# MoE input rows stored with the columns 8 apart side by side; pair 0 alone gathered on TensorE, pair 1 fetched by DMA

## The chip, the cores and the metric

One core of a Trainium2 chip runs the whole program. The metric is device microseconds of one execution; smaller is better.

## What is computed

The reference is a trunk of two decoder layers over 512 tokens of 1024 features in float32. Each layer has a token mixer and then a mixture of experts (MoE). The change lies in the MoE, cut here to what matters:

```
h  = rmsnorm(x) * (1 + scale) + shift            # (512, 1024), scale and shift from the conditioning
group  = argmax of 4 group logits                # top-1 group
expert = top-2 of the 8 experts in that group, weights by softmax
for each chosen expert e:                        # 32 experts, hidden width 256
    y += weight * (silu(h @ w_gate[e]) * (h @ w_up[e])) @ w_down[e]
x = x + gate * y
```

Every token goes to two of 32 experts, so an expert sees some 32 of the 512 tokens.

## The kernel before

**Tiling.** The tokens are four tiles of 128 (NT = 4). The feature axis is 8 chunks of 128 (NK = 8): feature d = 8q + k belongs to chunk k on partition q, which is the order in which the expert weights lie in memory. Every expert has 64 slots for its rows, two experts make a pair, and a pair's 128 slots fill the partitions. There are 16 pairs a layer, counted from 0.

**Routing.** `mix_out` runs the last stage of the mixer tile by tile and, woven into it, the router: `route_turn` and `route_mm` (logits), `route_sum` (L1478 and L1480, the logits turned), `route_pick` (L1499 to L1517, the chosen experts, `sel`), `route_rank` (L1524 and L1525, each row's place within its expert), `route_place` (L1530 and L1569, a 0/1 matrix `P` of token against slot), `route_send` (L1538 to L1547, the token number is written to a list in memory), `route_scale` (POOL, L1446: `h` = x times a row of factors), `route_halves` (L1607 and L1608: norm and shift). For the last of the four tiles these steps stand in an order written out by hand (L1389 to L1414).

**Two ways to the input of a pair.** Pairs 0 and 1 get their input `X` from TensorE: `gather_tile` multiplies `h` of each token tile, 8 column-strided chunks as the stationary operand, with `P` of four experts (256 columns moving), adding up over the tiles in four PSUM banks (L1588); ACT copies these to `X` (L1663). The other pairs are fetched: `fetch` clears a tile `raw` on POOL (L1629) and issues an indirect DMA that collects the pair's rows (L1630); `turn` transposes them on TensorE, eight 128x128 blocks read with a stride of 8 columns (L1712), and ACT copies them to `X` (L1713). One `fetch(h)` brings two pairs, 2h and 2h+1, and is called when `turn` has used up the earlier two. Before the first fetch the lists of token numbers are read back (`idx`, L1558).

**The pairs.** `gate_up(n)` (L1728) is 32 matmuls in two halves of the feature axis, followed by the activation (DVE L1737 to L1743, ACT L766 to L770). `down(n)` (L1763) is 16 matmuls, the scaling on DVE (L1766) and a scatter by POOL (L1776), or for the last pairs an addition on the chip (L1769 to L1804). The loop does `gate_up(n)`, `down(n-1)`, `turn(n+1)`. Behind `gate_up(0)` stands `overflow`, a conditional branch for experts with over 64 rows: every engine takes part in it, and none of its body is executed here. Instructions of SP that stand behind it are issued once SP has passed it.

**Loads.** Weights come through SP in the order of `plan_loads`: for pair 0 `gu`, pair 1 `gu`, pair 0 `dn`, pair 2 `gu`, pair 1 `dn` and so on (`gu` = the gate and up weights in four 1 MB tiles, `dn` = the down weights in two). All large tiles, weights, `X` and `raw`, share one pool of 19 buffers of 1 MB that is used in rotation, so each load waits for the release of the tile 19 allocations earlier. Up to the branch 16 weight tiles are loaded: pairs 0, 1 and 2 `gu`, pairs 0 and 1 `dn`. The loads behind it take, in this order, three buffers of pair 0's `gu`, then those of pair 1's `gu` and of the first `X`, then pair 0's `dn`. Near the end of a layer the rows that were scattered are loaded back (`yt`) between pair 14's and pair 15's weights.

## Time and profile before

| | |
|---|---|
| median of 3 runs | 1343.57 us (1343.27 to 1343.91) |
| the profiled execution | 1342.48 us, of which the span of the trace is 1340.7 us |
| mean granted TensorE clock | 0.941 of full speed |
| busy share of the span | PE 87%, PE weight loads 54%, DVE 54%, ACT 30%, POOL 27% |
| bytes moved | 350.95 MB, mean 262 GB/s |
| gate and up matmuls, L1728 | 260.0 us in 1024 instructions |
| gather matmuls, L1588 | 35.1 us in 128 instructions |
| transposes of fetched rows, L1712 | 33.8 us in 224 instructions (groups of four) |

The first layer's MoE runs from about 405 to 681 us of the span, the second's from about 1052 to 1326 us. A share of the span says little here, because the mixer and the MoE have different limits; the readings that matter are taken inside the two MoE stages, at their start and their end.

### The profile page before, as it was taken

How to read it: one execution, taken by the hardware profiler on the slowest of the kernel's cores; microseconds unless marked ns; L12 is line 12 of the kernel's file. 1: busy time of each engine (PE TensorE's matmuls, PEld its weight loads, DVE VectorE, ACT ScalarE, POOL GpSimd, SP SyncE). 2: the span in 40 equal slices, each digit the busy share in tenths (PEclk: the TensorE clock that was granted, in tenths of full speed). 3: DMA queues.
4: the chain of work that ended last, by engine and by line, in shares of the span. 5: the costliest groups of instructions: out<-in, count | busy, mean ns of one | idle time of the engine just before them, and what ended most of it. 6: DMA issues, size and time to landing. Idle time of an engine off the chain costs nothing. (4 is left out here: it accounts for less than half of the span.)

```text
span 1340.7 us, 16646 instructions
## 1 busy us (share of the span) xinstructions
PE 1164.4 (87%) x5900; PEld 728.2 (54%) x5902; DVE 719.9 (54%) x1573; ACT 401.6 (30%) x1029; POOL 358.0 (27%) x302
## 2 busy tenths in 40 slices
PE   4888899999988997788859998999998999888795
PEld 2766566666764553344337765767576644334342
DVE  3786877776662121124676576887777321112276
ACT  3442422545322111111134333345352121111113
POOL 0251322461232121111052313346132321111100
PEclk9898989989989999999979997989999999888898
DMA  9973256462877999999962220463385899999982
GB/s 379 400 276 116 75 189 225 145 228 56 312 237 267 411 413 410 405 398 411 393 225 95 75 95 30 176 219 111 107 273 209 247 412 413 412 411 404 398 336 79
DMA packets 104860, 350.95 MB, mean 262 GB/s; under 512 B 16874, under 2 KB 27882, under 8 KB 90434
## 3 DMA queue, kind: packets, MB, share of 16 engines
q1 hardware_dynamic: 85936, 313.31, 61.5%
q10 hardware_dynamic: 10738, 22.24, 4.8%
q0 software_dynamic: 8096, 14.24, 2.9%
q8 instruction: 51, 0.84, 0.3%
q14 instruction: 39, 0.32, 0.1%
HBM read 333.35 MB, written 29.48 MB: 271 GB/s over the span
## 5 line engine op out<-in xcount | busy, mean ns | idle before, releaser
L1728 PE MATMUL pa<-w,X 128*64 128x512 f32 x1024 | 260.0, 610 | 43.3 <-DMA w<-w_up 35.2
L1728 PEld LDWEIGHTS pa<-w,X 128*64 128x64 f32 x1024 | 102.2, 139 | 163.9 <-issue 119.5
L1763 PE MATMUL pb<-w,hT 128*64 128x512 f32 x512 | 142.7, 658 | 11.1 <-ACT hT L1752 10.7
L736 PE MATMUL pa<-wp,hhi 128*128 128x512 f32 x320 | 136.3, 429 | 3.5 <-ACT hhi L638 3.4
L737 PE MATMUL pa<-wp,hhi 128*128 128x512 f32 x320 | 131.7, 412 | 0.9 <-DVE wp L241 0.9
L738 PE MATMUL pa<-wp,hlo 128*128 128x512 f32 x320 | 130.1, 408 | 0.8 <-DVE hlo L639 0.8
L1737 DVE TENSOR_SCALAR sg<-pa 128x256 f32<-128x256 f32 x32 | 13.6, 424 | 201.9 <-PE pa L1728 201.9
L241 DVE TENSOR_TENSOR wp<-w,wp 128x1024 fp32r<-128x1024 f32 (+1 forms) x68 | 90.1, 1333 | 36.5 <-ACT wp L240 36.1
L1776 POOL DMA_INDIRECT yd<-y,idx x24 | 24.0, 1000 | 308.9 <-DVE y L1766 246.6
L240 ACT ACTIVATE wp<-w 128x1024 fp32r<-128x1024 f32 (+1 forms) x72 | 72.2, 1014 | 97.7 <-PE pa L738 44.7
L1763 PEld LDWEIGHTS pb<-w,hT 128*64 128x64 f32 x512 | 49.4, 149 | 80.3 <-issue 52.7
L1713 ACT ACTIVATE X<-pa 128x512 f32<-128x512 f32 x56 | 31.9, 598 | 171.8 <-PE pa L1712 157.8
L736 PEld LDWEIGHTS pa<-wp,hhi 128*128 128x128 f32 x320 | 63.0, 198 | 28.3 <-issue 6.5
L766 ACT ACTIVATE sge<-sg 128x256 f32<-128x256 f32 x32 | 13.2, 413 | 204.2 <-DVE sg L1737 204.2
L1766 DVE TENSOR_TENSOR y<-pb,gbc 128x512 f32<-128x512 f32 x48 | 33.2, 692 | 76.3 <-PE pb L1763 58.1
L738 PEld LDWEIGHTS pa<-wp,hlo 128*128 128x128 f32 x320 | 63.1, 197 | 17.0 <-issue 1.7
L737 PEld LDWEIGHTS pa<-wp,hhi 128*128 128x128 f32 x320 | 63.2, 198 | 15.2 <-DVE wp L241 1.9
L915 POOL TENSOR_TENSOR QX<-E,qk 128x1024 f32<-128x1024 f32 x16 | 40.9, 2559 | 98.4 <-ACT E L913 59.0
L1335 PE MATMUL pa<-wp,mlo 128*128 128x512 f32 x128 | 51.9, 406 | 1.0 <-DVE mlo L1307 1.0
L1333 PE MATMUL pa<-wp,mhi 128*128 128x512 f32 x128 | 52.6, 411 | 0.2
L931 PE MATMUL pb<-QX,E 64*128 64x128 f32 x448 | 43.5, 295 | 9.6 <-DVE hkg L1008 5.3
L1334 PE MATMUL pa<-wp,mhi 128*128 128x512 f32 x128 | 51.1, 399 | 0.0
(350 smaller groups left out, 2185.6 us busy)
## 6 DMA issues: line engine op xcount, KB each, us to landing
w<-w_gate SPq DMA_DIRECT2D x128, 512.0 KB, 13.8
w<-w_up SPq DMA_DIRECT2D x128, 512.0 KB, 7.6
w<-w_down SPq DMA_DIRECT2D x64, 1024.0 KB, 11.3
w<-w_ada SPq DMA_DIRECT2D x48, 1024.0 KB, 10.2
w<-w_in SPq DMA_DIRECT2D x16, 1024.0 KB, 6.8
w<-w_in SPq DMA_DIRECT2D x16, 512.0 KB, 7.0
yd<-Sblk SPq DMA_DIRECT2D x8, 1024.0 KB, 17.9
w<-w_out SPq DMA_DIRECT2D x8, 1024.0 KB, 6.3
```

The lines of the kernel that those rows point to most:

```text
L240: keep(self.S.activation(hi, w[:, sl, :], AF.Copy))
L241: keep(self.lo_engine.tensor_tensor(lo, w[:, sl, :], hi.bitcast(F32), op=OP.subtract))
L736: T.matmul(acc[i], hh[:, s], wh, start=k == 0, stop=False)
L737: T.matmul(acc[i], hh[:, s], wl, start=False, stop=False)
L738: T.matmul(acc[i], hl[:, s], wh, start=False, stop=k == NK - 1)
L915: G.tensor_tensor(qx, e, qk[i][:, pr, None, :].to_broadcast([P, 8, P]), op=OP.mult)
L931: T.matmul(o, e[r, lv, :], qx[r, lv, :], start=True, stop=True)
L1333: T.matmul(acc, mh[kh][:, kk, s], hi[:, kk % 2, :], start=first, stop=False)
L1334: T.matmul(acc, mh[kh][:, kk, s], lo[:, kk % 2, :], start=False, stop=False)
L1335: T.matmul(acc, ml[kh][:, kk, s], hi[:, kk % 2, :], start=False, stop=last)
L1728: mm = T.matmul(p[j * 64:j * 64 + 64, :], X[h][:, kh * 4 + kk, ep * P + j * 64:ep * P + j * 64 + 64], w[j][:, :, kk], start=kh == 0 and kk ...
L1763: T.matmul(p[j * 64:j * 64 + 64, :], hT[:, f, j * 64:j * 64 + 64], w[j][:, f, cs], start=f == 0, stop=f == 1)
```

## The change

Row storage: `h` is written in the order "k q" instead of "q k", so that the 128 columns of a chunk lie side by side. `route_scale` does the turning on POOL: it reads x and the factors with a stride of 8 columns, in runs of 64, and writes side by side. The shift row is turned once a layer by a new ACT copy of 128x1024 (`shift`), which takes a fifth buffer of the tag that holds the four `h`. The gather's stationary operand and the transposes of fetched rows then read 128 neighbouring columns.

Pairs: only pair 0 goes through the gather. `P` has 128 columns, there are two PSUM banks and two copies to `X`, and two opening matmuls instead of four. Pair 1 is fetched: `fetch(r)` brings pairs 2r+1 and 2r+2, clears both halves first and issues both DMAs behind that; the last fetch brings pair 15 alone. There are 15 gathers of rows a layer instead of 14. `down(0)` stands right behind the branch, before `turn(1)`, instead of behind `gate_up(1)`. In the written order of the last tile, `route_sum` stands before `gather_tile(0)`, and `gather_tile(2)` behind `route_send` of the last tile. The loads of pair 0's `dn` move ahead of pair 1's `gu`.

```diff
-                if e0 > 0:
-                    for e in (e0 - 2, e0 - 1):
-                        self.plan(("dn", l, e))
+                for e in (0, 1) if e0 == 0 else (e0 - 2, e0 - 1) if e0 > 2 else ():
+                    self.plan(("dn", l, e))
...
         self.route_rank(last - 1)
+        self.route_sum(last)
         self.gather_tile(0)
-        self.route_sum(last)
         self.route_pick(last)
...
         self.route_rank(last)
-        self.gather_tile(2)
         self.route_place(last)
         self.route_group(last)
         self.route_send(l, last)
+        self.gather_tile(2)
         self.gather_tile(last)
...
+        self.shift = self.t4([P, D], F32, "shift")
+        self.S.activation(self.shift.rearrange("p (k q) -> p k q", k=NK), self.rows[:, 0].rearrange("p (q k) -> p k q", k=NK), AF.Copy)
...
-        self.G.tensor_tensor(self.h[i][:, cs], self.xt[i][:, cs], self.rows[:, 1, cs], op=OP.mult)
+        h, x, s = self.h[i][:, cs], self.xt[i][:, cs], self.rows[:, 1, cs]
+        if self.turned:
+            h = self.h[i].rearrange("p (k q) -> p k q", k=NK)[:, :, half * 64:half * 64 + 64]
+            x, s = (t.rearrange("p (q k) -> p k q", k=NK) for t in (x, s))
+        self.G.tensor_tensor(h, x, s, op=OP.mult)
...
-        hv = self.h[i].rearrange("p (q k) -> p k q", k=NK)
         for k in range(NK):
-            o = self.pg[k // 2][:, (k % 2) * 256:(k % 2) * 256 + 256]
-            self.keep(self.T.matmul(o, hv[:, k], self.P0[i // 2][:, i % 2], start=False, stop=i == NT - 1 and k % 2 == 1))
+            o = self.pg[k // 4][:, (k % 4) * P:(k % 4) * P + P]
+            self.keep(self.T.matmul(o, self.h[i][:, k * P:k * P + P], self.P0[:, i], start=False, stop=i == NT - 1 and k % 4 == 3))
...
-        def fetch(h):
-
-            raw[h] = self.u([P, 2, D], F32, "raw")
-            for ep in range(2):
-                keep(G.memset(raw[h][:, ep], 0.0))
+        def fetch(r):
+
+            raw[r] = self.u([P, 2, D], F32, "raw")
+            pairs = [n for n in (2 * r + 1, 2 * r + 2) if n < NE // 2]
+            for j in range(len(pairs)):
+                keep(G.memset(raw[r][:, j], 0.0))
+            for j, n in enumerate(pairs):
                 ins = keep(G.indirect_dma_start(
-                    out=raw[h][:, ep], out_offset=None, in_=self.hd[l],
-                    in_offset=bass.IndirectOffsetOnAxis(ap=self.idx[:, 2 * h + ep, 0:1], axis=0),
+                    out=raw[r][:, j], out_offset=None, in_=self.hd[l],
+                    in_offset=bass.IndirectOffsetOnAxis(ap=self.idx[:, n, 0:1], axis=0),
...
                 self.overflow(l, *over)
                 self.reserve = 1
                 self.pump()
-            if n > 0:
+                down(0)
+            if n > 1:
                 down(n - 1, got)
             if n == NE // 2 - 2:
                 collect((0, 1))
-            if 1 < n + 1 < NE // 2:
+            if n + 1 < NE // 2:
                 turn(n + 1)
```

What the scheduler makes of it can be read from the order of the instructions on an engine. A row is a line of the kernel it stands in, the operation, and out<-in with buffer numbers.

PE at the end of the first layer's routing, before. `sel` is the last tiles' chosen experts, `lgT` the logits of the last tile, `P` the token and slot matrices, `h` the rows, `pa` the banks of the gather:

```order
L1525 MATMUL pb_3349<-sel_2962,low_419 128x32
L1588 MATMUL pa_3318<-P_2966,h_2927 128x256 x2
L1588 MATMUL pa_3320<-P_2966,h_2927 128x256 x2
L1588 MATMUL pa_3322<-P_2966,h_2927 128x256 x2
L1588 MATMUL pa_3342<-P_2966,h_2927 128x256 x2
L1480 MATMUL pb_3362<-late_65,lgT_2959 128x40
L1588 MATMUL pa_3318<-P_2966,h_2928 128x256 x2
L1588 MATMUL pa_3320<-P_2966,h_2928 128x256 x2
L1588 MATMUL pa_3322<-P_2966,h_2928 128x256 x2
L1588 MATMUL pa_3342<-P_2966,h_2928 128x256 x2
L1524 LDWEIGHTS onesb_421
```

The same place now, up to the first row of the rank of the last tile:

```order
L1530 MATMUL pb_3344<-sel_2963,low_419 128x32
L1485 MATMUL pb_3349<-late_65,lgT_2960 128x40
L1591 MATMUL pa_3317<-P_2967,h_2928 128x128 x4
L1591 MATMUL pa_3319<-P_2967,h_2928 128x128 x4
L1591 MATMUL pa_3317<-P_2967,h_2929 128x128 x4
L1591 MATMUL pa_3319<-P_2967,h_2929 128x128 x4
L1529 LDWEIGHTS onesb_421
```

The logits of the last tile (L1480, now L1485) have moved ahead of the first tile's gather. In both kernels the second tile's gather stands before the rank of the last tile, and the third and fourth behind it; a tile's gather has 8 instructions in both, of 256 and now of 128 columns.

PE behind the branch in the first layer, before: `gate_up(1)` at once (L1728), then `hid` of pair 0 turned (L1750), then `turn(2)` (L1712) and `down(0)` (L1763):

```order
L1857 UNCONDITIONAL_BRANCH
L1728 MATMUL pa_3793<-w_2910,X_3317 64x512
...
L1728 MATMUL pa_3793<-w_3458,X_3317 64x512
L1750 MATMUL pb_3831<-first_64,sg_3541 128x128 x2
L1712 MATMUL pa_3859<-first_64,raw_3476 128x128 x4
L1712 MATMUL pa_3865<-first_64,raw_3476 128x128 x4
L1763 MATMUL pb_3837<-w_3461,hT_3834 64x512
```

The same place now (L1718 is `turn`, L1735 `gate_up`, L1757 `hid` turned, L1770 `down`):

```order
L1865 UNCONDITIONAL_BRANCH
L1718 MATMUL pa_3815<-first_64,raw_3473 128x128 x4
L1718 MATMUL pa_3821<-first_64,raw_3473 128x128
L1757 MATMUL pb_3788<-first_64,sg_3536 128x128 x2
L1718 MATMUL pa_3821<-first_64,raw_3473 128x128 x3
L1735 MATMUL pa_3827<-w_3021,X_3316 64x512
L1770 MATMUL pb_3794<-w_2910,hT_3791 64x512
...
L1735 MATMUL pa_3827<-w_3453,X_3316 64x512
```

`turn(1)` is the first work behind the branch, and `down(0)`, although it is written ahead of `turn(1)`, stands behind the first matmul of `gate_up(1)`. The second layer has the same order.

ACT ahead of the branch, before; it ends with the copies to `X` (L1663) and the branch's counter:

```order
L1663 ACTIVATE X_3317<-pa_3318 128x512
L1663 ACTIVATE X_3317<-pa_3320 128x512
L1663 ACTIVATE X_3317<-pa_3322 128x512
L1663 ACTIVATE X_3317<-pa_3342 128x512
L1856 TENSOR_LOAD cnti_3524
L1857 COMPARE_AND_BRANCH
```

And now:

```order
L1668 ACTIVATE X_3316<-pa_3317 128x4x128
L1668 ACTIVATE X_3316<-pa_3319 128x4x128
L765 ACTIVATE sge_3538<-sg_3536 128x256
L768 ACTIVATE sge_3538<-sge_3538 128x256
L769 ACTIVATE sge_3538<-sge_3538 128x256
L1864 TENSOR_LOAD cnti_3519
L1865 COMPARE_AND_BRANCH
```

The three steps of pair 0's activation stand ahead of the branch now, where they stood behind it. On POOL the two clears and the two row fetches stand ahead of the branch in both.

## Rows read from the trace of the kernel before

**Rows 1.** Waits of PE for weights, second MoE stage (us, times, longest):

```profile
PE pa L1728 <- DMA w<-w_up: 15.4, 6, 3.2
```

**Rows 2.** Stretches of the second MoE stage: busy by engine, clock, DMA share, GB/s:

```profile
1057.00:1060.00 3.00, 3.00 (x16) 0.86 (x12) 0.00 (x0) 0.38 (x1) 2.19 (x2) 1.00 0.24 5
1060.00:1066.00 6.00, 5.51 (x25) 1.60 (x23) 1.43 (x6) 1.25 (x3) 3.05 (x3) 1.00 0.70 230
1066.00:1072.00 6.00, 5.19 (x25) 1.74 (x26) 0.36 (x1) 0.00 (x0) 0.00 (x0) 1.00 0.83 208
1100.00:1150.00 50.00, 45.19 (x206) 22.66 (x204) 9.41 (x18) 8.34 (x21) 7.00 (x7) 0.93 1.02 412
```

**Rows 3.** Timeline of PE, second layer: end of routing, first pairs (start, duration, instruction):

```profile
1040.47 4.18 PE L1588 MATMUL pa<-P,h 128*128 128x256 f32 x16
1044.49 0.31 PE L1480 MATMUL pb<-late,lgT 128*128 128x40 f32 x2
...
1048.74 8.01 PE L1588 MATMUL pa<-P,h 128*128 128x256 f32 x32
1056.67 3.65 PE L1728 MATMUL pa<-w,X 128*64 128x512 f32 x16
```

**Rows 4.** Groups of PE's weight loads: the gather's, and one of side-by-side columns:

```profile
L1588 PEld LDWEIGHTS pa<-P,h 128*128 128x128 f32 x128 | 32.4, 335 | 3.9 <-POOL h L1446 2.8
L1655 PEld LDWEIGHTS pb<-late,P 128*128 128x128 f32 x64 | 8.7, 191 | 1.6 <-DVE P L1651 0.9
```

**Rows 5.** Timelines of POOL and DVE, second layer, end of routing:

```profile
1039.06 1.28 POOL L1446 TENSOR_TENSOR h<-x,rows 128x512 f32<-128x512 f32 x1
...
1061.70 1.08 POOL L1630 DMA_INDIRECT raw<-hd,idx  x1 [2.46 <-issue]
...
1038.48 1.92 DVE L1517 TENSOR_TENSOR sel<-o 128x32 bf16<-128x32 f32 x1
...
1046.90 0.19 DVE L1517 TENSOR_TENSOR sel<-o 128x32 bf16<-128x32 f32 x1
```

**Rows 6.** Timeline of SP's queue: first load behind the branch (both layers), and later ones:

```profile
1065.81 0.34 SPq L216 DMA_DIRECT2D w<-w_gate  x1
...
419.07 0.35 SPq L216 DMA_DIRECT2D w<-w_gate  x1
...
425.69 0.33 SPq L216 DMA_DIRECT2D w<-w_gate  x1
...
637.12 0.33 SPq L216 DMA_DIRECT2D w<-w_gate  x1
...
1283.91 0.33 SPq L216 DMA_DIRECT2D w<-w_gate  x1
```

**Rows 7.** DMA issues of fetched rows (count, median us to landing): 1055 to 1075 us, then all:

```profile
raw<-hd,idx POOLq DMA_INDIRECT x2, 4.8
...
raw<-hd,idx POOLq DMA_INDIRECT x28, 7.7
```

**Rows 8.** Timelines of DVE and ACT: the activation behind one pair's gate and up:

```profile
1258.09 0.42 DVE L1737 TENSOR_SCALAR sg<-pa 128x256 f32<-128x256 f32 x1 [5.43 <-PE pa L1728]
...
1259.57 0.42 ACT L770 ACTIVATE sge<-sge 128x256 f32<-128x256 f32 x1
```

**Rows 9.** Timeline of PE, ends of both MoE stages: pairs 13 to 15:

```profile
642.30 0.65 PE L1728 MATMUL pa<-w,X 128*64 128x512 f32 x1 [3.41 <-DMA w<-w_up]
...
643.21 5.26 PE L1763 MATMUL pb<-w,hT 128*64 128x512 f32 x15
...
1262.76 1.52 PE L1712 MATMUL pa<-first,raw 128*128 128x128 f32 x6 [4.28 <-DMA raw<-hd,idx]
1264.21 5.21 PE L1763 MATMUL pb<-w,hT 128*64 128x512 f32 x16
...
1289.11 0.61 PE L1728 MATMUL pa<-w,X 128*64 128x512 f32 x1 [2.00 <-ACT sge L770]
...
1289.72 3.87 PE L1763 MATMUL pb<-w,hT 128*64 128x512 f32 x15
```

More of the change, by code (lines that the diff above doesn't have):

```diff
@@ L649, in next_open @@
         self.h = {i: z[i // 2][:, i % 2, :] for i in range(NT)}
-        self.ssq, self.r = {}, {}
+        self.ssq, self.r, self.turned = {}, {}, False
     def next_hT(self, l):
@@ L1390, in mix_out @@
         self.pin = True
-        self.gather_open(0, 3)
+        self.gather_open(2)
         h = self.route_turn(last, 1)
@@ L1491, in route_top @@
         self.etop = self.dtl([P, NT, 8], F32, "etop")
-        self.P0 = [self.t2([P, 2, 256], F32, "P") for _ in range(2)]
+        self.P0 = self.t2([P, NT, P], F32, "P")
         self.one, self.ei, self.sent, self.hsent, self.ysent = {}, {}, [], [], []
@@ L1530, in route_place @@
         self.V.scalar_tensor_tensor(self.sp[:, i], self.prank, 1.0, self.sel[:, i], op0=OP.add, op1=OP.mult)
-        self.place(self.P0, 0, i)
+        self.place(i)
     def route_send(self, l, i):
@@ L1565, in route_group, with place, gather_open @@
         self.S.activation(ge, ge, AF.Exp, accum_out=self.gsum[:, i:i + 1])
-    def place(self, Ph, h, i):
-        self.V.tensor_tensor(Ph[i // 2][:, i % 2].rearrange("p (e s) -> p e s", e=4),
-                             self.c["iota"][:, None, :].to_broadcast([P, 4, CAP]),
-                             self.sp[:, i, h * 4:h * 4 + 4, None].to_broadcast([P, 4, CAP]), op=OP.is_equal)
-    def gather_open(self, a, b):
-        if a == 0:
-            self.X0 = self.u([P, NK, 256], F32, "X")
-            self.pg = []
+    def place(self, i):
+        self.V.tensor_tensor(self.P0[:, i].rearrange("p (e s) -> p e s", e=2),
+                             self.c["iota"][:, None, :].to_broadcast([P, 2, CAP]),
+                             self.sp[:, i, 0:2, None].to_broadcast([P, 2, CAP]), op=OP.is_equal)
+    def gather_open(self, n):
+        self.X0 = self.u([P, NK, 256], F32, "X")
+        self.pg = []
         zero = self.low[:, 0:1].to_broadcast([P, P])
-        for _ in range(a, b):
+        for _ in range(n):
             p = self.pa()
@@ L1596, in route_tile @@
     def route_tile(self, i):
-        h, sh = self.h[i], self.rows[:, 0]
+        h, sh = self.h[i], self.shift
         self.V.scalar_tensor_tensor(h, h, self.r[i], sh, op0=OP.mult, op1=OP.add)
@@ L1605, in route_halves @@
             cs = slice(half * 512, half * 512 + 512)
-            h, sh = self.h[i][:, cs], self.rows[:, 0, cs]
+            h, sh = self.h[i][:, cs], self.shift[:, cs]
             self.keep(S.activation(h, h, AF.Copy, scale=self.r[i]))
@@ L1658, in places @@
             wsl[2 * h], wsl[2 * h + 1] = w[:, 0:1], w[:, 1:2]
-        fetch(1)
+        fetch(0)
         X[0] = self.X0
-        for g in range(4):
-            keep(S.activation(X[0][:, g * 2:g * 2 + 2, :], self.pg[g].rearrange("p (k s) -> p k s", k=2), AF.Copy))
+        for g in range(2):
+            keep(S.activation(X[0][:, g * 4:g * 4 + 4, 0:P], self.pg[g].rearrange("p (k s) -> p k s", k=4), AF.Copy))
         w1 = self.tiny([P, NT], F32, "w1")
@@ L1705, in turn @@
             h, ep = n // 2, n % 2
-            rows = raw[h][:, ep].rearrange("p (q k) -> p q k", k=NK)
+            r, j = (n - 1) // 2, (n - 1) % 2
+            rows = raw[r][:, j].rearrange("p (k q) -> p k q", k=NK)
             if ep == 0:
@@ L1711, in turn @@
                 for k in range(4):
-                    T.transpose(p[:, k * P:k * P + P], rows[:, :, g * 4 + k], self.ident)
+                    T.transpose(p[:, k * P:k * P + P], rows[:, g * 4 + k], self.ident)
                 S.activation(X[h][:, g * 4:g * 4 + 4, ep * P:ep * P + P], p.rearrange("p (k s) -> p k s", k=4), AF.Copy)
-            if ep == 1:
+            if n == NE // 2 - 1:
+                self.free()
+            elif j == 1:
                 self.live -= 1
-                if h + 1 < NH:
-                    fetch(h + 1)
+                fetch(r + 1)
         over, SIDE = [], {(0, 3): count}
```

7 lines of the change are left out of this document (3 added, 4 removed).

## The prediction

> **What bounds the kernel now.** I read four views, in this order: the waits of PE, the stretches of the MoE, the timelines at its start, the timelines at its end. In the second MoE stage PE waits six times for weights, 15.4 us in all [rows 1], so PE has slack there. The stretches say why: between 1100 and 1150 us the DMA engines are fully busy (share 1.02) at 412 GB/s [rows 2], a stream of weights that nothing on the chip can speed up. What can move is its beginning. From 1057 to 1060 us 5 GB/s flow, then 230 and 208 GB/s for 6 us each [rows 2]. Against 412 GB/s that is 3.0 + 2.7 + 3.0 = 8.7 us of lost full-rate time, because all tiles that fit are loaded and SP stands at the branch until 1065.81 us [rows 6]. So the first question is when SP passes the branch and how fast the buffers behind it come free; the speed of the gather is only a means to that.
>
> The second question is the end of the stage. At 1262.76 us PE has waited 4.28 us for the rows of pair 14 [rows 9], the largest single wait there. What follows it decides whether that wait is worth anything. In the first layer PE waits at `gate_up(15)` until 642.30 us for `w_up` [rows 9]. SP's loads run at a constant offset between the layers there: 637.12 against 1283.91 us, 646.79 us apart [rows 6]. So pair 15's first weights land at about 642.30 + 646.79 = 1289.09 us in the second layer, and `gate_up(15)` starts at 1289.11 us [rows 9]. ACT is named as its releaser, but the weights come at the same moment.
>
> The profiled execution took 1342.48 us, its span is 1340.7 us, and the median of the runs is 1343.57 us. I apply the differences worked out from the span to the median.
>
> **Gather and routing.** A tile's gather takes 4.18 us for 16 PE operations [rows 3], 0.26 us each, at a weight load of 335 ns; a load of side-by-side columns takes 191 ns [rows 4]. With 128 columns moving instead of 256, the lower bound is one load of 191 ns hidden in part behind the other, the upper 16 times 191 ns = 3.1 us a tile. L1655 has such weights with one column moving and paces at 133 to 191 ns, so I take 0.14 us times 16 = 2.2 us a tile. On the path: the logits' turn, L1480, starts at 1044.49 us only because it stands behind the first gather, and it can go at about 1042, 2.5 us earlier. The chain of picks behind it ends in `sel` at 1046.90 us [rows 5], now 1044.4. Gathers 0 and 1 end at about 1042.2 + 2 times 2.2 = 1046.6 us, and then the rank. Gathers 2 and 3, 8.01 us from 1048.74 before [rows 3], take 4.4 us and end near 1051.1. `gate_up(0)` would start at 1051.3 instead of 1056.67 us, 5.4 us earlier.
>
> Against it stands the strided `route_scale`. It takes 1.28 us contiguous, and the `sel` in its neighbourhood takes 1.92 us where the next tile's takes 0.19 [rows 5]; both end together, so DVE is held until POOL is done. No row shows POOL reading with a stride. The nearest is PE's load, 335 against 191 ns [rows 4], a factor of 1.75; the bounds are no cost and 1.28 times 0.75 = 1.0 us per operation, of which the last tile's and one ahead of it lie on this path, 0 to 2.0 us. I take 0.4 us, near the low end, since the row nearest to it is the same operation on the same engine. That leaves 5.0 us. The extra ACT copy of the shift lies beside the mixer's matmuls at each layer's start of routing; without that cover it would cost two copies of 0.6 us each, once a layer.
>
> [...]
>
> **The branch.** SP goes on when the slowest engine has arrived. Now three steps of pair 0's activation stand ahead of the branch on ACT. Behind an ordinary pair they end 1259.57 + 0.42 - 1258.09 = 1.9 us after the gate and up matmuls [rows 8]. With `gate_up(0)` from 1051.7 to 1059.0 us and some 1.2 us from the last engine to SP's first load, as now, SP would go on at 1062.1. POOL is later: its chain (rank, list of numbers, read back, first fetch at 1061.70 [rows 5]) starts some 1.5 us earlier, so the fetches are issued at about 1060.2 and 1061.3 (the clears stand ahead now) and end at 1062.4. SP then goes on near 1063.0 instead of 1065.81 us, a gain of 2.8 us; by the same steps 3.3 us in the first layer, from 419.07 [rows 6].
>
> **Pair 1's rows.** Here the time is given back. Pair 1 was ready when the branch was passed. Now its rows are fetched at 1060.2 us and, with the 4.8 us that the first two fetches took before [rows 7], and 0.5 us for the second beside it, land at about 1065.5. PE stands idle from 1059.0 until then, at a falling clock, and `turn(1)`, the first copy and the first matmul of `gate_up(1)` bring `down(0)` to about 1068 to 1072. That matters to the loads: the fourth and fifth load tiles behind the branch reuse pair 0's `dn`, where they reused pair 1's `gu` before, and the seventh reuses the first `X`, free only after `gate_up(1)`, at about 1080. Three tiles, 3.1 MB, last from about 1066 to 1074 at 412 GB/s. A load issued at 1072.3 with 2 us to flow leaves a gap of about 0.8 us; bounds 0, if rows land at 1064, and 3.5, if they take the 7.7 us that is the median of all fetches [rows 7]. In the first layer the fourth load has so far waited until 425.69 us [rows 6], for `gate_up(1)`, and would wait until about 425, so the gap there grows by less, 0.5 us. PE itself is 3 to 4 us late at `gate_up(2)`, which its 15.4 us of slack covers.
>
> **One more fetch.** A pair's rows are 512 times 2 / 16 = 64 rows of 4 KB, 0.26 MB, 0.64 us of the stream at 412 GB/s, per layer.
>
> **The end of a layer.** Pair 14's rows now come with pair 13's, one fetch earlier, and the waits of 4.28 us and its like in the first layer go. Nothing is won by that alone, since pair 15's first weights are what `gate_up(15)` meets next, at 642.30 and about 1289.09 us less what the stream gains. In the second layer the idle time moves behind `turn(15)` and gets longer, and the clock with it: after its idle time in the first layer `down(13)` took 5.26 us, in the second, with less, 3.87 [rows 9]. I charge the difference and the slow matmul beside it, 1.6 us (0 to 1.8). Pair 15's fetch stands behind POOL's work for `down(12)`, a whole `gate_up(14)` before its use, and I charge nothing for it.
>
> **The sum.** Second layer: -2.8 (branch) + 0.8 (gap) + 0.64 (fetch) + 1.6 (clock) = +0.2. First layer: -3.3 (branch) + 0.64 (fetch) + 0.5 (gap) = -2.2. Together -2.0 us: 1343.57 - 2.0 = 1341.6, say 1341.5 us. Everything else of the 10 us by which the two `gate_up(0)` start earlier is spent on waiting for pair 1.
>
> **The rivals.** *A, the end pays as well.* If pair 15's weights land earlier than the offset says, because SP's loads there no longer wait for PE, the 4.28 us of [rows 9] count and no clock is lost: -1.4 and -2.2 for the streams, -4.3 for the wait: about 1335.7 us; half of the wait would give 1338. For it speaks that ACT is named as releaser at 1289.11; against it the agreement within 0.02 us.
>
> *B, pair 1 starves the stream.* If its rows land after about 1066.5 us, `down(0)` on a slow clock (5.21 us behind the wait at 1262.76 [rows 9], not 3.9) ends after 1074, and the three tiles have run dry. With a gap of 3.5 us in each layer: second -2.8 + 3.5 + 0.64 + 1.6 = +2.9, first -3.3 + 3.5 + 0.64 = +0.8: about 1347.3 us, slower; the point of no gain lies at a gap of some 2 us in both. For it speaks that PE now has nothing to do but wait; against it that these two fetches meet nearly empty DMA queues.
>
> *C, the gather does not speed up,* because POOL's strided reads hold DVE for the full 2.0 us or PE's loads stay near 335 ns. Then `gate_up(0)` starts 2.5 to 3.5 us earlier, but POOL's chain, not it, sets the branch, and about 1 us of the gain is lost in each layer: 1343.5 us, no change.
>
> **How the numbers follow.** What a measurement of this kernel can tell from no change is about 0.2%, 2.7 us: faster is under 1340.9, slower over 1346.2. The forecast has 0.48 with its own range of 1339.5 to 1343.5 (0.20 of it faster, 0.28 the same), A 0.20 (faster), B 0.22 (slower mostly, 0.02 the same), C 0.10 (the same): faster 0.40, same 0.40, slower 0.20. The range leaves out the full A and the full B: 1336.5 to 1346.5 us.
>
> **What would show it.** Right: `gate_up(0)` near 1051.5 us, SP's first load behind the branch near 1063 and 416, a wait of PE for `raw` of about 6 us at `turn(1)`, no wait at `turn(14)`, and a wait for `w_up` at `gate_up(15)` in both layers. The gather shows in weight loads near 190 ns, POOL in the duration of `route_scale` (1.3 or 2 us). It is wrong if the fourth load behind the branch comes more than 2 us after the third has flowed (B), or if `gate_up(15)` starts before 1286 us (A).

## The result, and the profile after

The changed kernel takes 1365.31 us (median of 4 runs, 1362.89 to 1368.01); the kernel before took 1343.58 us beside it (1343.27 to 1343.91). The ratio is 1.0162, with a 95% interval of 1.0146 to 1.0179: 21.7 us slower, where 1341.5 was forecast and 1346.5 was the upper end. The profiled execution of after took 1368.01 us with a span of 1366.2, so its trace shows 25.5 us more than that of before, about 2.7 more than a median run.

The start of the second MoE stage, where [rows 2] lost 8.7 us of full-rate time, now looks like this (stretches: length, busy time of PE, PEld, DVE, ACT and POOL with their instructions, granted clock, DMA share, GB/s):

```profile
core 0: us, PE busy (x) PEld busy (x) DVE busy (x) ACT busy (x) POOL busy (x), PEclk, DMA share, GB/s
1072.00:1077.00 5.00, 4.49 (x22) 1.15 (x18) 0.95 (x4) 0.00 (x0) 0.00 (x0) 1.00 0.89 284
1077.00:1081.00 4.00, 0.00 (x0) 0.00 (x0) 0.85 (x2) 1.25 (x3) 3.08 (x3) 1.00 0.33 55
1081.00:1091.00 10.00, 0.00 (x0) 0.00 (x0) 0.00 (x0) 0.00 (x0) 2.08 (x2) 0.51 0.86 280
1091.00:1096.00 5.00, 4.88 (x20) 2.95 (x22) 0.00 (x0) 1.58 (x3) 0.00 (x0) 0.61 0.40 159
1096.00:1099.00 3.00, 3.00 (x18) 1.30 (x17) 0.96 (x2) 0.00 (x0) 0.00 (x0) 1.00 0.00 0
1099.00:1102.00 3.00, 3.00 (x18) 1.36 (x16) 0.42 (x1) 0.00 (x0) 1.02 (x1) 1.00 0.73 195
1102.00:1150.00 48.00, 40.48 (x189) 19.62 (x187) 7.87 (x16) 9.26 (x23) 9.75 (x10) 0.96 1.02 404
```

PE does nothing from 1077 to 1091 us, the clock granted to it is 0.51 of full speed in the idle stretch from 1081 to 1091 us, and behind that the stream of weights itself runs dry: 159, 0 and 195 GB/s. Against the 412 GB/s of [rows 2] the stretch 1091 to 1102 loses 3.1 + 3.0 + 1.6 = 7.7 us of the stream. From 1102 us on the stream is as full as before.

The timeline of PE in the same stage (start, duration, instruction, wait before it), the answer to [rows 3] and the last rows of [rows 9]:

```profile
1065.36 3.82 PE L1591 MATMUL pa<-P,h 128*128 128x128 f32 x32
1069.10 3.65 PE L1735 MATMUL pa<-w,X 128*64 128x512 f32 x16
1072.84 3.65 PE L1735 MATMUL pa<-w,X 128*64 128x512 f32 x16
1091.12 1.30 PE L1718 MATMUL pa<-first,raw 128*128 128x128 f32 x5 [14.63 <-DMA raw<-hd,idx]
1094.34 3.87 PE L1770 MATMUL pb<-w,hT 128*64 128x512 f32 x14
...
1312.61 1.09 PE L1735 MATMUL pa<-w,X 128*64 128x512 f32 x1 [6.49 <-DMA w<-w_up]
...
1313.65 5.50 PE L1770 MATMUL pb<-w,hT 128*64 128x512 f32 x15
```

The gather of two tiles fell from 8.01 to 3.82 us, as the plan wanted, and yet `gate_up(0)` starts at 1069.10 us, not at 1056.67. `turn(1)` then waits 14.63 us for pair 1's rows, and 13.26 us in the first layer. Why the rows come so late is in the timelines of POOL and of SP's queue, the answer to [rows 5, 6]:

```profile
1077.11 1.22 POOL L1563 DMA_DIRECT2D idx<-idd  x1 [7.69 <-issue]
...
1081.90 1.08 POOL L1635 DMA_INDIRECT raw<-hd,idx  x1 [1.71 <-issue]
1083.29 0.99 POOL L1635 DMA_INDIRECT raw<-hd,idx  x1 [0.30 <-issue]
...
1081.17 0.33 SPq L216 DMA_DIRECT2D w<-w_gate  x1
...
1083.85 0.73 SPq L216 DMA_DIRECT2D w<-w_up  x1
1098.68 0.33 SPq L216 DMA_DIRECT2D w<-w_gate  x1
```

SP's six loads of 0.5 MB behind the branch (a tile of 1 MB is two of them) go out from 1081.17 us, ahead of the two fetches at 1081.90 and 1083.29. The rows then take 9.2 us from the first fetch's issue to `turn(1)`. SP's seventh load, the first of the prediction's fourth tile, waits until 1098.68 us, because its buffer is released only behind `down(0)`. In the first layer the same load waits 15.4 us, by the trace for PE's `down(0)` (L1770):

```profile
SPq L216 <- PE pb L1770: 15.4, 1, 15.4
```

The rest of the difference sits ahead of `gate_up(0)`. The group of the strided `route_scale`, and one of these with the DVE instruction that overlaps it:

```profile
L1451 POOL TENSOR_TENSOR h<-x,rows 128x512 f32<-128x512 f32 x16 | 32.7, 2046 | 58.0 <-DVE x L1341 58.0
```

```profile
394.74 2.70 DVE L1512 SCALAR_TENSOR_TENSOR mk<-no,mk 128x32 f32<-128x32 f32 x1
...
395.37 2.01 POOL L1451 TENSOR_TENSOR h<-x,rows 128x512 f32<-128x512 f32 x1
```

One operation takes 2046 ns on average where it took 1306, and DVE's 128x32 instruction, 0.19 us when alone, ends with it.

Starts cannot be taken from two traces as they stand: a mixer step of the first layer that stands ahead of every changed instruction of the routing, `gt<-pa`, already comes 1.7 us later in the trace of after. So starts are counted here from the first `y<-pa,gbc` of a layer's routing. In the first layer, before and then after (first mixer step, first and last `y<-pa,gbc`, `gate_up(0)`):

```profile
311.54 0.69 DVE L869 TENSOR_SCALAR gt<-pa 128x512 f32<-128x512 f32 x1
350.04 0.69 DVE L1341 TENSOR_TENSOR y<-pa,gbc 128x512 f32<-128x512 f32 x1 [1.08 <-PE pa L1335]
385.85 0.68 DVE L1341 TENSOR_TENSOR y<-pa,gbc 128x512 f32<-128x512 f32 x1
409.68 3.65 PE L1728 MATMUL pa<-w,X 128*64 128x512 f32 x16
```

```profile
313.25 0.69 DVE L868 TENSOR_SCALAR gt<-pa 128x512 f32<-128x512 f32 x1
351.77 0.69 DVE L1340 TENSOR_TENSOR y<-pa,gbc 128x512 f32<-128x512 f32 x1 [1.08 <-PE pa L1334]
392.71 0.68 DVE L1340 TENSOR_TENSOR y<-pa,gbc 128x512 f32<-128x512 f32 x1
410.26 3.65 PE L1735 MATMUL pa<-w,X 128*64 128x512 f32 x16
```

The mixer's seven steps from the first `y<-pa,gbc` to the last take 35.8 us before and 40.9 after, 5.1 more (3.6 more in the second layer). From the first one to `gate_up(0)` it is 59.6 us before and 58.5 after, so `gate_up(0)` comes 1.2 us earlier in the first layer, and 0.4 us in the second (59.4 and 59.0). In the second layer the routing itself starts 12.8 us later, at 1010.14 instead of 997.30; with 1.7 of it there from the start, the first layer had lost some 11 us by then.

### The profile page after: what moved, and what is told of

Read it like the earlier page. It is cut to its first block, busy times and chain, and to the rows that moved or that the text cites. A ratio compares the mean times of both kernels' runs of the same rounds, so it can differ in the third digit from the quotient of the medians.

```text
span 1366.2 us, 16698 instructions
## 1 busy us (share of the span) xinstructions
PE 1150.1 (84%) x5912; PEld 726.3 (53%) x5914; DVE 731.5 (54%) x1573; ACT 406.4 (30%) x1031; POOL 372.4 (27%) x306
## 5 line engine op out<-in xcount | busy, mean ns | idle before, releaser
L1735 PE MATMUL pa<-w,X 128*64 128x512 f32 x1024 | 256.1, 607 | 16.1 <-DMA w<-w_up 11.5
L1735 PEld LDWEIGHTS pa<-w,X 128*64 128x64 f32 x1024 | 105.7, 139 | 123.0 <-issue 87.5
L1770 PE MATMUL pb<-w,hT 128*64 128x512 f32 x512 | 143.6, 651 | 2.7 <-ACT hT L1759 2.7
L1718 PE MATMUL pa<-first,raw 128*128 128x128 f32 x240 | 37.6, 306 | 69.9 <-DMA raw<-hd,idx 69.9
L1770 PEld LDWEIGHTS pb<-w,hT 128*64 128x64 f32 x512 | 49.8, 150 | 71.8 <-issue 53.7
L1718 PEld LDWEIGHTS pa<-first,raw 128*128 128x128 f32 x240 | 30.3, 156 | 85.1 <-issue 76.9
L914 POOL TENSOR_TENSOR QX<-E,qk 128x1024 f32<-128x1024 f32 x16 | 40.9, 2558 | 98.6 <-ACT E L912 59.2
L1332 PE MATMUL pa<-wp,mhi 128*128 128x512 f32 x128 | 53.1, 415 | 0.4 <-ACT mhi L1305 0.2
```

The source lines that it names most:

```text
L914: G.tensor_tensor(qx, e, qk[i][:, pr, None, :].to_broadcast([P, 8, P]), op=OP.mult)
L1332: T.matmul(acc, mh[kh][:, kk, s], hi[:, kk % 2, :], start=first, stop=False)
L1718: T.transpose(p[:, k * P:k * P + P], rows[:, g * 4 + k], self.ident)
L1735: mm = T.matmul(p[j * 64:j * 64 + 64, :], X[h][:, kh * 4 + kk, ep * P + j * 64:ep * P + j * 64 + 64], w[j][:, :, kk], start=kh == 0 and kk ...
L1770: T.matmul(p[j * 64:j * 64 + 64, :], hT[:, f, j * 64:j * 64 + 64], w[j][:, f, cs], start=f == 0, stop=f == 1)
```

## Experiments

These runs were made on other chips than the first comparison. The kernel before had medians of 1343.1 to 1344.8 us there too, but its single runs spread from 1335.6 to 1350.0, so each verdict is the ratio to before on the same chip, and one trace shows one execution of that spread. The first `y<-pa,gbc` of the first layer stands anywhere from 346.6 to 351.9 us in these traces, whatever the edit, so a start of `gate_up(0)` is compared by its distance from that step (59.6 and 59.4 us in the two layers before, 58.5 and 59.0 in the changed kernel).

**The row layout alone, both pairs gathered as before.** The edit to the kernel before; the gather, `shift` and the transposes follow the layout in hunks not shown here:

```diff
-        self.G.tensor_tensor(self.h[i][:, cs], self.xt[i][:, cs], self.rows[:, 1, cs], op=OP.mult)
+        h = self.h[i].rearrange("p (k q) -> p k q", k=NK)[:, :, half * 64:half * 64 + 64]
+        x, s = (t.rearrange("p (q k) -> p k q", k=NK) for t in (x, s))
+        self.G.tensor_tensor(h, x, s, op=OP.mult)
```

> The kernel before with the row storage changed alone: strided route_scale on POOL, the shift row turned by ACT, gather and transposes of fetched rows on neighbouring columns; pairs 0 and 1 are both gathered, and the order of the last tile, of the loads and of the fetches is that of before. Theory P (each of the 8 strided route_scale a layer holds DVE 0.74 us longer, and all 8 lie on the chain of the routing): gate_up(0) comes 8 x 0.74 = 5.9 us later a layer, less what the faster gather gives back (16 PE operations a tile instead of 4.2 us some 3 us, two tiles on the path: 2 us): +4 us a layer in the routing, and so +4 to +8 us in all, 1348 to 1352. Rival Q (only the fetch of pair 1 costs): the faster gather wins and the time is 1338 to 1343.5.

Measured: 1352.92 us, ratio 1.0068 (1.0036 to 1.0100), 9 us slower, just above Theory P's range and far from rival Q's. POOL took 2042 ns an operation. The gather of two tiles took 7.15 us, only 0.9 less than before, and `gate_up(0)` came 3.2 and 5.3 us later than before, counted from the layer's first `y<-pa,gbc`. The layout costs by its reads and gives almost nothing while 256 columns move.

**The pairs alone: pair 0 gathered, pair 1 fetched, rows stored as before.**

```diff
-            h = self.h[i].rearrange("p (k q) -> p k q", k=NK)[:, :, half * 64:half * 64 + 64]
-            x, s = (t.rearrange("p (q k) -> p k q", k=NK) for t in (x, s))
-        self.G.tensor_tensor(h, x, s, op=OP.mult)
+        self.G.tensor_tensor(self.h[i][:, cs], self.xt[i][:, cs], self.rows[:, 1, cs], op=OP.mult)
...
+        hv = self.h[i].rearrange("p (q k) -> p k q", k=NK)
-            self.keep(self.T.matmul(o, self.h[i][:, k * P:k * P + P], self.P0[:, i], start=False, stop=i == NT - 1 and k % 4 == 3))
+            self.keep(self.T.matmul(o, hv[:, k], self.P0[:, i], start=False, stop=i == NT - 1 and k % 4 == 3))
```

> The changed kernel with the row storage of before: route_scale is contiguous, gather and transposes read columns 8 apart; pair 0 alone is gathered, pair 1 is fetched, loads, fetches and order as in the changed kernel. Theory P (the late rows of pair 1 come from the late routing and what it pushes behind the weight loads): route_scale back at 1.3 us, idx read back near 408 instead of 417 us, pair 1's rows at 418 to 420 us, time 1342 to 1350. Rival Q (pair 1's fetch starves the stream whenever it is fetched): PE still waits over 10 us for the rows at turn(1), and the time stays over 1357.

Measured: median 1353.24 us, ratio 1.0086 (1.0054 to 1.0118), in five runs from 1342.32 to 1360.57. The median lies between the two ranges named, so neither theory is borne out for all runs. The layout alone and the pairs alone cost 0.68% and 0.86%, 1.54% in all, and the whole change 1.62%. The gather of two tiles took 7.90 us in the second layer and 7.86 in the first: with a stride, 128 columns save 0.11 and 0.15 us against the 8.01 of 256. The profiled execution is the fastest of the five, and it shows the other outcome of the race (PE, POOL and SP's queue, second layer):

```profile
1065.49 1.30 PE L1713 MATMUL pa<-first,raw 128*128 128x128 f32 x5 [3.81 <-DMA raw<-hd,idx]
...
1061.74 1.08 POOL L1630 DMA_INDIRECT raw<-hd,idx  x1 [2.38 <-issue]
...
1063.71 0.33 SPq L216 DMA_DIRECT2D w<-w_gate  x1
...
1072.65 0.33 SPq L216 DMA_DIRECT2D w<-w_gate  x1
```

Here the fetch goes out 2.0 us ahead of SP's first load (2.7 in the first layer), and the rows are used 3.75 us after its issue. That is the order that the prediction had taken for certain. The slower runs of this kernel have no trace, so that they lost this race is not shown.

**The stride moved from the reads to the write.** The changed kernel, with `route_scale` reading side by side and writing with the stride:

```diff
-            h = self.h[i].rearrange("p (k q) -> p k q", k=NK)[:, :, half * 64:half * 64 + 64]
-            x, s = (t.rearrange("p (q k) -> p k q", k=NK) for t in (x, s))
+            h = self.h[i].rearrange("p (k q) -> p q k", k=NK)[:, half * 64:half * 64 + 64]
+            x, s = (t.rearrange("p (q k) -> p q k", k=NK) for t in (x, s))
```

> The changed kernel, but route_scale reads x and the factors side by side and writes h with a stride of 8 columns, so the same rows are stored with the stride on the other side. If POOL's price is one of reading: 1.3 us an operation, routing and pair 1's rows as early as in the run with the pairs alone, and the faster gather on top: 1340 to 1348. If any stride costs: 1.9 to 2.1 us an operation and the time of the changed kernel, 1363 to 1368.

Measured: 1356.7 us, ratio 1.0097 (1.0072 to 1.0122), 8.7 us better than the changed kernel (1.0162 - 1.0097, of 1344; by the two intervals some 4 us either way), and above the 1340 to 1348 that was expected for a price of reading. POOL's group, and the first layer's first `y<-pa,gbc` and `gate_up(0)`:

```profile
L1451 POOL TENSOR_TENSOR h<-x,rows 128x512 f32<-128x512 f32 x16 | 20.7, 1296 | 58.3 <-DVE x L1341 57.8 <-DVE gtop L1506 0.6
...
349.63 0.69 DVE L1340 TENSOR_TENSOR y<-pa,gbc 128x512 f32<-128x512 f32 x1 [1.08 <-PE pa L1334]
...
401.78 3.65 PE L1735 MATMUL pa<-w,X 128*64 128x512 f32 x16
```

With the stride on the write POOL takes 1296 ns, against 1306 without any and 2046 with it on the reads, so the whole price of the operation is one of reading. `gate_up(0)` comes 52.2 us after the first `y<-pa,gbc`, 7.5 us earlier than in the kernel before (6.1 in the second layer), and 6.3 us earlier than in the changed kernel (5.7 in the second layer). Eight operations that are each 0.75 us shorter make 6.0 us: all eight of a layer lie on the path. The race is lost none the less:

```profile
1078.87 1.30 PE L1718 MATMUL pa<-first,raw 128*128 128x128 f32 x5 [14.56 <-DMA raw<-hd,idx]
...
1070.23 1.08 POOL L1635 DMA_INDIRECT raw<-hd,idx  x1 [2.53 <-issue]
...
1067.83 0.33 SPq L216 DMA_DIRECT2D w<-w_gate  x1
```

**No wait for pair 1.** The changed kernel with pair 1 computed on pair 0's input and `turn(1)` left out; pair 1's rows are still fetched, and not used.

```diff
-            for g in range(2):
+            for g in range(2 if n > 1 else 0):
...
-                        mm = T.matmul(p[j * 64:j * 64 + 64, :], X[h][:, kh * 4 + kk, ep * P + j * 64:ep * P + j * 64 + 64],
+                        mm = T.matmul(p[j * 64:j * 64 + 64, :], X[h][:, kh * 4 + kk, (ep if n != 1 else 0) * P + j * 64:(ep if n != 1 else 0) * P + j * 64 + 64],
```

> The changed kernel, with pair 1 computed on pair 0's input: turn(1) is left out, so nothing waits for pair 1's rows, which are fetched all the same. Theory S (down(0) stands behind that wait on PE, the fourth load behind the branch reuses its buffers, and the stream stops for 7 to 8 us in each layer): the fourth load comes within 8 us of the first, the stop goes, 1348 to 1354. Rival R (the loss is the late start of the MoE alone, and the wait lies in PE's slack): 1360 to 1366.

Measured: 1350.55 us, ratio 1.0044 (1.0028 to 1.0060). SP's seventh load behind the branch comes at 426.47 and 1077.10 us instead of 439.18 and 1098.68. The wait is worth (1.0162 - 1.0044) of 1344 = 15.9 us (by the two intervals some 3 us either way), the larger part of the loss, as Theory S has it.

**The written order alone** (`route_sum` ahead of `gather_tile(0)` in the kernel before).

```diff
-        self.gather_tile(0)
         self.route_sum(last)
+        self.gather_tile(0)
```

> The kernel before, with one line of the change: route_sum of the last tile ahead of gather_tile(0). Nothing else differs, POOL is contiguous and pairs 0 and 1 are both gathered. Theory (the branch opens at the end of gate_up(0), and the stream of weights restarts with it, as long as pair 2's rows are not needed before they land): gate_up(0) and SP's first load behind the branch come 2 to 2.6 us earlier in each layer, and the time falls by 2 to 5 us, 1339 to 1342. Rival (the list of token numbers and its read-back set the start, not PE): no change, 1343 to 1344.5.

Measured: 1345.71 us, ratio 1.0023 (1.0006 to 1.0040), just above the rival's range and no gain. Counted from the layer's first `y<-pa,gbc`, `gate_up(0)` came 0.8 and 2.6 us later than before. The logits' turn did go earlier, but then two gathers run together, and the last tile's rank starts behind them no earlier. No gain lies in the order while a gather of two tiles takes 8 us.

**Weights held back until the rows are there**, once without the layout and once in the changed kernel. The first load behind the branch waits for the fetches of pairs 1 and 2:

```diff
+                if getattr(self, "first", None):
+                    self.behind(ins, self.first)
+                    self.first = None
```

> The run with the pairs alone, in which the first weight load behind the branch also waits until the rows of pairs 1 and 2 have landed. Its times ran from 1342 to 1361. Theory W (the spread is a race: SP's loads go on when gate_up(0) ends, POOL's fetch goes when the lists have been read back, and whoever comes second waits behind the other in the DMA engines; 3 MB of weights are 7.6 us): with the fetch always first, the times lie within 5 us of each other and under 1348, and PE's wait at turn(1) is under 6 us in both layers. Rival (the spread has to do with something else, or rows are late for another reason): spread of over 10 us as before.

> The changed kernel, in which the first weight load behind the branch also waits until the rows of pairs 1 and 2 have landed. Theory W: rows of pair 1 land some 4 to 5 us after their fetch instead of 8.5, turn(1) and down(0) come 3.5 us earlier in each layer, and the stream runs without the stop before the fourth load although it starts 6 us later: 1356 to 1362. Rival (the order in the DMA engines is not the matter): 1363 to 1372, since the loads start later.

Measured: 1352.67 us, ratio 1.0071 (1.0048 to 1.0095), without the layout; its six runs lie within 7 us (1350.3 to 1357.4; within 5 was expected), where the five of the pairs alone lay within 18. With the layout 1363.24 us, ratio 1.0135 (1.0111 to 1.0158), in the rival's range. `turn(1)` waits 4.19 and 3.58 us without the layout, within what was expected, and 8.20 and 9.50 with it, since there the fetches themselves are issued late. POOL and PE in the first layer of the run with the layout:

```profile
421.24 1.08 POOL L1638 DMA_INDIRECT raw<-hd,idx  x1 [1.90 <-issue]
...
425.11 1.30 PE L1724 MATMUL pa<-first,raw 128*128 128x128 f32 x5 [8.20 <-DMA raw<-hd,idx]
```

From issue to use the rows now take 3.9 us (3.6 in the second layer), where they take 8.6 and 9.2 in the changed kernel, so the order in the DMA engines does decide when they land. The level was expected lower in both runs: the hold removes the queue in front of the rows and moves SP's restart back, to 423.44 us without the layout and 427.58 with it, instead of 419.07 before and 420.35 in the changed kernel. What the rows gain the weights lose.

**The layout by a strided write, both pairs gathered, the logits' turn first.** The kernel before with the strided write shown above and the order shown above.

> The kernel before with the rows stored in the changed order, but by a route_scale that reads side by side and writes with a stride, with gather and transposes on neighbouring columns, both pairs gathered, and route_sum ahead of gather_tile(0). Theory: gate_up(0) comes 4 to 6 us earlier in each layer, nobody waits for pair 1, and pair 2's rows are wanted only a gate_up later; SP's loads restart 4 to 6 us earlier: 1334 to 1340. If the fetch of pair 2's rows then falls behind the restarted loads, turn(2) waits some 3 us, which PE has in hand. Rival (the token lists set the pace whatever the gather does): 1341 to 1344.

Measured: 1343.86 us, ratio 0.9995 (0.9978 to 1.0011): no change, as the rival has it. Two tiles take 7.15 us again. The four cases of the gather of two tiles, behind each of which the first 16 matmuls of `gate_up(0)` take 3.65 us, are then 8.01 us (256 columns, strided), 7.15 (256, side by side), 7.86 (128, strided) and 3.82 (128, side by side). Either half of the change leaves the other limit standing.

**Pair 1 gathered by a second pass on TensorE** instead of a fetch, so that nothing waits for a DMA. The kernel before with the strided write, 128 columns for pair 0, the changed order of the last tile (`route_sum` first, `gather_tile(2)` behind `route_send`), and behind `gate_up(0)`, ahead of the branch:

```diff
+                self.gather_open(1)
+                for i in range(NT):
+                    self.gather_tile(i, 1)
+                self.gather_copy(1)
                 self.overflow(l, *over)
```

> The layout written with a stride and read contiguously, pair 0 gathered alone with 128 columns, and pair 1 not fetched: TensorE gathers it in a second pass of 4 tiles x 8 matmuls behind gate_up(0), ahead of the branch. The loads, the fetches of the later pairs and the order of the turns are those of before. Theory (the gain of a short gather is real, and the change loses it and more because pair 1's rows stand behind weights): gather of two tiles 3.8 us, gate_up(0) 5 to 7 us earlier than 409.68 and 1069.1, no wait of TensorE for rows at turn(1), first load behind the branch up to 5 us earlier, 1332 to 1340 us. Rival (the end is set by when SP restarts the weights, and SP's restart does not follow gate_up(0)): gate_up(0) as early, first load behind the branch at 415 to 418 as before, 1342 to 1346 us.

Then the same with the matmul that counts the overflow put first, and the kernel before with this edit alone:

```diff
-        over, SIDE = [], {(0, 3): count}
+        over, SIDE = [], {(0, 0): count}
```

> As the run with the second pass, with the matmul that counts the experts' overflow (on whose result the branch is taken) at the first step of gate_up(0) instead of its last. If SP's restart follows that count, the first load behind the branch comes about 3 us earlier than in the second-pass run, and the time falls by up to 6 us (3 a layer); if SP follows the end of gate_up(0) or the other engines' arrival, nothing moves.

> The kernel before with that count alone moved to the first step of gate_up(0). If SP's restart follows the count: first load behind the branch 2 to 3 us earlier than 415.64 and 1065.81, and 1338 to 1342 us. If SP is tied to something else: 1343 to 1345 us, no change.

And the first of them with the pass on the far side of the branch:

```diff
                 self.overflow(l, *over)
                 self.reserve = 1
                 self.pump()
+                self.gather_open(1)
+                for i in range(NT):
+                    self.gather_tile(i, 1)
+                self.gather_copy(1)
```

> The run with the second pass, with the pass moved behind the branch: TensorE takes the branch right after gate_up(0) and gathers pair 1 on the far side of it, while weights stream. (To free the buffers that the rows need across the branch, the branch's body, which this input never takes, loads its weights into one buffer in turn instead of into three.) In the second-pass run SP's third load behind the branch waited 7.4 and 4.0 us for TensorE at the branch. Theory (SP's restart is tied to TensorE's passage of the branch, which the second pass held up): third load at 411 to 413 instead of 418.65, the stream saturated some 5 us earlier in each layer, 1332 to 1339 us. Rival (the stream is limited by something else there, such as the code behind the branch): third load at 416 to 419, 1342 to 1346 us.

Measured: 1344.60 us with the pass ahead of the branch, ratio 1.0017 (1.0000 to 1.0034). With the count of the overflow first as well, 1347.27, ratio 1.0031 (1.0014 to 1.0048); the kernel before with the count first, 1345.22, ratio 1.0007 (0.9990 to 1.0024). With the pass behind the branch, 1342.41, ratio 0.9986 (0.9967 to 1.0005). In the first of them `gate_up(0)` started at 399.67 us, counted from the first `y<-pa,gbc` 6.6 us earlier than before (5.9 in the second layer), and the time did not move. All four lie in the rivals' ranges, where one was given, or within 1 us of it. The waits of SP's queue around the start of the first layer's MoE, and PE's second pass:

```profile
SPq L216 <- PEq L1868: 7.4, 1, 7.4
```

```profile
407.50 7.30 PE L1592 MATMUL pa<-P,h 128*128 128x128 f32 x64
419.15 8.83 PE L1735 MATMUL pa<-w,X 128*64 128x512 f32 x32 [4.35 <-PEq L1868]
```

SP's first two loads go at 410.31, but the third waits 7.4 us, for PE's branch by the trace, which stands behind the second pass. Behind the branch (the last of these runs) all six go from 414.33 us, but the pass now delays `gate_up(1)`:

```profile
414.14 8.29 PE L1592 MATMUL pa<-P,h 128*128 128x128 f32 x60 [2.34 <-issue]
422.37 7.09 PE L1735 MATMUL pa<-w,X 128*64 128x512 f32 x32
...
426.05 0.33 SPq L216 DMA_DIRECT2D w<-w_gate  x1
```

SP's seventh load needs a buffer that `gate_up(1)` frees and comes at 426.05, against 425.69 in [rows 6]. SP's third load came at 415.32 in that run, ahead of the rival's 416 to 419 and behind the theory's 411 to 413. The count is not what SP follows: with it first in the kernel before, SP's first load came 8.3 us after the count instead of 5, and 2.6 us after the end of `gate_up(0)` instead of 2. What SP does follow is not shown.

**Both losses out at once.** The changed kernel with the strided write and without the wait for pair 1 (pair 1 computed on pair 0's input, as above). It leaves the earlier `gate_up(0)` alone.

> The changed kernel with the stride on the write and with pair 1 computed on pair 0's input (turn(1) left out, its rows still fetched): both losses taken out at once, so that what is left is the earlier gate_up(0) alone. Sum of the single runs: from 1365.3, minus 8.6 (stride on the write) and minus 14.8 (no wait) = 1342, no change against before. Theory (an earlier start of gate_up(0) hardly reaches the end, since the stream is restarted by the branch and filled by the buffers that gate_up(1) frees): 1339 to 1345. Rival (the two losses hid a gain of 5 to 7 us a layer that the plan would have brought): 1330 to 1336.

Measured: 1340.57 us, ratio 0.9976 (0.9960 to 0.9992). PE and SP's queue, second layer:

```profile
1049.42 3.65 PE L1735 MATMUL pa<-w,X 128*64 128x512 f32 x16
...
1282.96 1.08 PE L1735 MATMUL pa<-w,X 128*64 128x512 f32 x1 [7.51 <-DMA w<-w_up]
...
1284.00 5.33 PE L1770 MATMUL pb<-w,hT 128*64 128x512 f32 x15
...
1059.94 0.33 SPq L216 DMA_DIRECT2D w<-w_gate  x1
...
1065.00 0.33 SPq L216 DMA_DIRECT2D w<-w_gate  x1
```

Against the changed kernel this is 1.0162 - 0.9976 = 1.86%, 25.0 us, and the two single runs add up to 8.7 + 15.9 = 24.6, within their intervals the same. So these two account for the loss, and what is left with both out is a gain of 3.2 us (1.1 to 5.4), within Theory's range. Counted from the layer's first `y<-pa,gbc`, `gate_up(0)` starts 7.5 us earlier than before in the first layer and 6.1 in the second, `gate_up(15)` 1.0 and 5.0 us.

## Why the prediction was wrong

**What bounds the kernel** was read rightly: the stream of weights, and when it restarts behind the branch. After the stalls it ran at 404 GB/s, and six waits of PE for fetched rows in that stretch (1102 to 1305 us), up to 4.9 us long, did not slow it:

```profile
PE pa L1718 <- DMA raw<-hd,idx: 20.5, 6, 4.9
```

**The gather** was sized too low in its gain (2.2 us a tile forecast, 3.82 us for two measured) and rightly said to be a means only. From the last `y<-pa,gbc` to `gate_up(0)` the first layer took 17.6 us instead of 23.8, 6.3 less before rounding.

**The strided `route_scale` is the first step that failed.** The prediction took 0.4 us on the path in all, "since the row nearest to it is the same operation on the same engine", and counted two operations. The operation took 0.74 us more (2046 against 1306 ns, a factor of 1.57), near the 1.0 of PE's strided load [rows 4], which was the upper bound. And all eight of a layer lie on the path, not two: reading side by side instead gave back 6.3 us in the first layer and 5.7 in the second, 8 times 0.75 being 6.0. Beside seven of a layer's eight operations DVE has an instruction that ends 0.01 to 1.08 us after POOL's (`x<-y,x` takes 1.78 and 2.00 us there, and 0.69 alone), and DVE's chain of norm, picks and mixer sets the pace of the routing. What holds DVE there no run shows: L1512's row (2.70 us) opens 0.63 us ahead of POOL's (2.01) and ends 0.06 us behind it. In the first layer 5.1 of the 6.3 us that the gather gave back went there, in seven steps of the mixer, and `gate_up(0)` came 1.2 us earlier instead of 5. The trace of before showed this hold (`sel` at 1.92 instead of 0.19 us, [rows 5]), and the prediction used it for the last tile's operation and one ahead of it alone. In time this step was worth 8.7 us. The extra ACT copy of the shift took 2.3 us, not two copies of 0.6, but off the path as said: from the mixer's `gt<-pa` to the first `y<-pa,gbc` it is 38.5 us in both traces.

**The branch is the second.** "SP goes on when the slowest engine has arrived", with POOL's fetches as the slowest, put the rows ahead of the weights by construction. Its 1.2 us "from the last engine to SP's first load, as now" stands in no row: in the second layer before, it was 0.8 us from the end of POOL's last fetch and 1.75 from the end of `gate_up(0)`. SP does not wait for POOL's fetches: its first load went at 420.35 and 1081.17 us, ahead of the fetches at 422.27 and 1081.90. In the kernels that do not hold the loads back it came 1.8 to 6.1 us after the end of `gate_up(0)`. Counted from the layer's first `y<-pa,gbc`, the gain of 3.3 and 2.8 us at the branch became a gain of 0.4 us in the first layer and a loss of 2.5 in the second.

**Pair 1's rows are the third, and the largest.** The mechanism was rival B, "pair 1 starves the stream", with its place and its sign; the size was off, and its own time of 1347.3 us is still 18 us short of the measured one. The gap was put at 0.8 and 0.5 us, with 3.5 as its upper bound from the median landing of all fetches [rows 7]. Two things had been left out. The token lists and their reading back now meet preloaded weights: the last list goes out at 409.60 us (before 404.97), from 408 to 414 us 414 and 346 GB/s are still flowing where 6 and 5 GB/s flowed before, and POOL waits 6.53 us for the list in place of 3.01. Why these weights flow so late is not shown; the late routing alone does not do it, for with the strided write the last list goes out at 401.12 us and POOL still waits 8.31 us. And the fetch, once behind SP's six loads, meets 3 MB of weights: 8.6 and 9.2 us from issue to use, against 3.75 in the run that won the race. `down(0)` ended at 1098.64 us instead of at some 1072, and the stream lost 7.7 us in the second layer and, by the same arithmetic from 431 to 444 us, 8.9 in the first: 16.6 in all, near the 15.9 that the run without the wait gave back. Putting the rows first does not mend it, as the runs with the held weights show: whichever of the two goes first, the other waits.

**The end of the layer** came as forecast. The wait at pair 14 is gone and brought nothing; pair 13, whose rows now come with pair 14's, waits instead, 2.09 and 2.53 us. PE waits for `w_up` at `gate_up(15)` in both layers (2.13 and 6.49 us); `down(13)` behind it runs at 5.50 instead of 3.87 us, 1.6 us as charged.

**The sum.** That -2.0 us lies near the -3.2 of the run without both losses is a coincidence. That run has no price of reading and no wait at `turn(1)`, where the prediction charged for both; its earlier start is worth 7.5 and 6.1 us at `gate_up(0)`, and in the first layer 1.0 us of it is left at `gate_up(15)`. There SP needs 6.1 us from the end of `gate_up(0)` to its first load, and 2.0 in the kernel before. The waits of SP's queue in that stretch (404 to 428 us):

```profile
SPq L1865 <- SPq L1865: 7.6, 3, 4.5
```

The trace puts the waits to SP's own branch. Four DMA packets that it counts as instructions move from 408.5 to 414.6 us; whether SP waits for them no run here tested. What sets the restart stays open.

## What to carry to other kernels

When a DMA-fed input takes the place of a computed one, find out which transfers will be issued ahead of it on the path to memory. Here a small gather behind 3 MB of weights took 9 us, not 4. Who wins that race may change from run to run: the 18 us spread of the pairs alone, 7 when the weights were held, speaks for it, but no slow run was traced. Price an operation on an engine that blocks another by the blocked engine's chain, and count every instance on that chain. And before paying for an earlier start, take the losses away in an experiment and see what the start is worth: here 3.2 us (1.1 to 5.4), with `gate_up(0)` 7.5 and 6.1 us earlier in the two layers.

## What the runs showed of the hardware

POOL's 128x512 float32 product took 1306 ns with reads and write side by side, 2042 to 2046 with a read stride of 32 bytes, and 1296 with a write stride of 32 bytes. TensorE's float32 gather of two tiles took 8.01, 7.15, 7.86 and 3.82 us for the four combinations of load and columns, so here either a strided weight load or 256 moving columns was enough to keep it above 7 us. A gather of a pair's rows, 0.26 MB, was used 3.6 to 3.9 us after its issue where it went ahead of SP's six loads and the rows ended the wait, and 8.6 to 9.2 us after it in the changed kernel, behind them. In the changed kernel SP passed the branch without waiting for POOL's fetches (its first load at 420.35 us, the first fetch at 422.27), and with a second pass of PE's ahead of the branch its third load waited 7.4 us for PE's branch by the trace.
